# Six of the 24 pieces of a conditioning matrix taken among the first four projection groups of a two-block transformer kernel

## The chip, the cores and the metric

One core of one Trainium2 chip runs the whole program. The metric is device time in microseconds (us) of one execution, as the median of several runs. Its engines are TensorE (PE, with its weight loads listed apart as PEld), VectorE (DVE), ScalarE (ACT), GpSimd (POOL) and SyncE (SP), whose queue issues nearly all weight transfers. Each engine works through its own queue in order.

## The reference, cut to what matters

256 tokens of width 1024 pass through two blocks in fp32. The first block has an attention mixer and a linear attention (HGRN2), whose outputs are merged, and a mixture of 32 experts. The second block has its own attention, a state-space layer and another 32 experts. What the change touches is how the second block is conditioned on one vector `c`, and the linear attention's forget gate in the first block:

```python
# second block: shifts, scales and gates from the conditioning vector
c_act = silu(c)                                   # 1024 values
mod = c_act @ w_ada + b_ada                       # [1024] x [1024, 6144]
sh1, sc1, g1, sh2, sc2, g2 = split(mod, 6)
h = rmsnorm(x, norm1_g) * (1 + sc1) + sh1         # used in the second block only
...
# first block: linear attention
f = lb + (1 - lb) * sigmoid(f_logit)
log_f, k = log(f), 1 - f
bcum = cumsum(log_f)                              # in chunks of 64 tokens
o = linear_attention(q * exp(bcum), k, v, bcum)
```

`mod` depends on `c` and `w_ada` alone, so its work can be done at any time before the second block.

## The kernel before, in words

**Weights.** `Slots` keeps 20 SBUF buffers of 1 MB. `W.get(key)` hands out a weight tile, `W.done(key)` gives it back and calls `W.pump()`, which starts further loads in the order of first use of the whole program, at most `W.ahead` tiles ahead (6 from L509, 3 from L747). All these loads go through SP's queue. At L1144 and L1199 the first block's mixers give their buffers back and the first experts' weights (`m1w`) are started.

**Order.** The program is written as one sequence; a scheduler in the compiler puts each engine's instructions into an order by priority and by its own idea of durations. The engines then run that order as it stands, so an instruction that turns out late holds what is queued behind it on its engine.

**The first column groups.** After the row norm and a transposition (L533 to L540, result `hTf`), the columns of `w_in` are projected in groups of 256: `f0 f1 hq0 hq1` (L649 to L666, forget gate and query of the linear attention), `hi0 hi1` (its values), `kva0 kva1 kvb0 q0 q1` (the attention's keys, values and queries), all as fp32 matmuls (L567, L576). `prep` fetches one group further than the one asked for. `hgg0 hgg1` and `m00` to `m31` follow as split matmuls (L464). `hg_prep` (L687) prepares operands of the linear attention on DVE, ACT and POOL; `hgrn` (L964) does its matmuls, with `level` (L990) producing `am` on DVE (L1004) and `back` (L1008) using it on PE (L1012). `nsa`, `hgrn` and `fill` are interleaved by `run_all` at L1138.

**The pieces.** `mod` is computed in 24 pieces of 256 columns. `ada(site)` (L587) is called at places of the program that have names; where the name is in `ADA_SITES` (L26) it first calls `ada_flush()` and then takes one piece with `ada_()` (L611) at a priority lowered by 100. A piece multiplies eight slabs of a 1 MB weight tile by the columns of `cact` (= silu(c)) and adds them: on ACT (eight scalings, L621) with three adds on POOL (L622 to L624), or, for the piece numbers in `ADA_DVE`, by eight operations on DVE alone (L616, L618). The sum goes to a tile `ada` with two buffers. `ada_flush` (L595) reduces it over partitions on PE (L602 for the first 16 pieces, L608 for the last 8) and adds the bias on DVE (L604, L609). The flush stands at normal priority at the next site, so a piece's last write waits for the flush of the piece two before it.

**`cact`.** `par2` holds `c` and other parameters; it is loaded behind the row norm (L506). At L655 to L660 `cact` is filled: a POOL copy that depends on the forget gate (L655), a POOL copy of `c`, a Tanh on ACT and two DVE operations. Before, the 24 sites begin with `hi0 hi1`, and pieces 14 to 19 go to DVE.

Of the kernel before, what the change touches and what calls it, by code (L numbers as in the profile page):

```python
# [10 lines left out]
F32 = mybir.dt.float32  # L11
BF = mybir.dt.bfloat16
I32 = mybir.dt.int32
AF = mybir.ActivationFunctionType
OP = mybir.AluOpType
# [7 lines left out]
WB = 20  # L23
CAP1 = 32
CAP2 = 64
ADA_SITES = ("hi0 hi1 kva0 kva1 kvb0 q0 q1 cmpk cmpv hgg0 hgg1 m20 m21 m30 m31 m00 m01 m10 m11 bh0 bh2 bh4 bh6 bn0").split()  # L26
ADA_DVE = range(14, 20)

# [182 lines left out]
def view(tile_, spec_at, name):  # L213
    o, w = spec_at[name]
    return tile_[:, o:o + w]
# [94 lines left out]
def program(ctx: ExitStack, tc, T, out, plan):  # L310
    nc = tc.nc
    R32 = mybir.dt.float32r

    tt, ts, stt = nc.vector.tensor_tensor, nc.vector.tensor_scalar, nc.vector.scalar_tensor_tensor
    act, mm, tr = nc.scalar.activation, nc.tensor.matmul, nc.tensor.transpose
# [58 lines left out]
    par1 = cpool.tile([128, p1n], F32, name="par1")  # L374
    P1 = lambda n: view(par1, p1at, n)
    par2 = cpool.tile([128, p2n], F32, name="par2")
    P2 = lambda n: view(par2, p2at, n)
# [6 lines left out]
    def evac(o, i, scale=None, n=256):  # L384

        a, v = 0.22 + n / 1400.0, 0.07 + n / 960.0
        if eng_bal[0] + a <= eng_bal[1] + v:
            eng_bal[0] += a
            if scale is None:
                nc.scalar.copy(o, i)  # L390
            else:
                act(o, i, AF.Copy, scale=scale)
        else:
            eng_bal[1] += v
            if scale is None:
                nc.vector.tensor_copy(o, i)
            else:
                ts(o, i, scale, None, op0=OP.mult)
# [73 lines left out]
    both = lambda t, f: [f(t[0]), f(t[1])]  # L472


    W.ahead = 1
    W.pump()
    f1x = ExitStack()
    f1c = f1x.enter_context(tc.tile_pool(name="f1c", bufs=1))
    fs = f1x.enter_context(tc.tile_pool(name="f1s", bufs=2))
    pp1 = f1x.enter_context(tc.tile_pool(name="ps1", bufs=8, space=PSUM))  # L480

    def ps():
        return pp1.tile([128, 512], F32, name="ps", tag="ps")

    cst1 = f1c.tile([128, c1n], F32, name="cst1")
    grow = cpool.tile([128, 512], F32, name="grow")
# [16 lines left out]
    r = [row_r(fs, x_sb[:, i], junk[:, i], f"n1{i}", i == 0) for i in range(2)]  # L503
    W.drop()

    for t, n in ((par1, "par1"), (cst1, "cst1"), (par2, "par2"), (grow, "bgate")):  # L506
        nc.gpsimd.tensor_copy(t[:, 0:1], r[0])
        (nc.scalar if n == "par1" else nc.sync).dma_start(t, T[n])
    W.ahead = 6  # L509
# [41 lines left out]
    def used(*names):  # L551
        for n in names:
            del sp[n]
            if n in whole:
                W.done(n)
            else:
                W.drop(2)
        W.pump()
# [10 lines left out]
    def pair_T(n):  # L569

        prep(n)
        p = ps().rearrange("p (a t) -> p a t", a=2)
        for a in range(2):
            for k in range(8):
                if n in whole:
                    mm(p[:, a], sp[n][:, k, 128 * a:128 * a + 128], hTf[:, k], start=a == 0 and k == 0, stop=k == 7, skip_group_check=True)  # L576
                else:
                    mm3(p[:, a], wk(n, k, 128 * a, 128), [hTp[0][:, k], hTp[1][:, k]], a == 0 and k == 0, k == 7)
        return p


    cact = cpool.tile([128, 8], F32, name="cact")
    modp = cpool.tile([128, 4, 8], F32, name="modp")
    ada_next = iter(range(24))
    ada_rest = []

    def ada(site):  # L587
        if site in ADA_SITES:
            ada_flush()
            with tc.high_priority(offset=-100):  # L590
                ada_()
        if site == "end":
            ada_flush()

    def ada_flush():  # L595
        while ada_rest:
            n, t, s = ada_rest.pop()
            v, j = ADA[n]
            p = ps()
            if v in ADA_COLS:  # L600
                for a in range(2):
                    mm(p[:, a:a + 1], t[:, 128 * a:128 * a + 128], s, start=(a == 0), stop=True, skip_group_check=True)  # L602
                c = 8 * ADA_COLS.index(v) + 2 * j
                tt(modp.rearrange("p v k -> p (v k)")[:, c:c + 2], p[:, :2], P2("bada")[:, c:c + 2], op=OP.add)  # L604
            else:
                r, c = 32 * (2 * (v // 5) + j // 2), 256 * (j % 2)
                r, c = slice(r, r + 32), slice(c, c + 256)
                mm(p[r, :256], s.to_broadcast([128, 32]), t, start=True, stop=True)  # L608
                tt(grow[r, c], p[r, :256], grow[r, c], op=OP.add)  # L609

    def ada_():  # L611
        n = next(ada_next)
        w = W.get(("ada", n)).rearrange("p (k c) -> p k c", k=8)
        t = fs.tile([128, 256], F32, name="ada", bufs=2)
        if n in ADA_DVE:
            ts(t, w[:, 0], cact[:, 0:1], None, op0=OP.mult)  # L616
            for k in range(1, 8):
                stt(t, w[:, k], cact[:, k:k + 1], t, op0=OP.mult, op1=OP.add)  # L618
        else:
            for k in range(8):  # L620
                act(w[:, k], w[:, k], AF.Copy, scale=cact[:, k:k + 1])  # L621
            nc.gpsimd.tensor_tensor(w[:, 0:4], w[:, 0:4], w[:, 4:8], op=OP.add)  # L622
            nc.gpsimd.tensor_tensor(w[:, 0:2], w[:, 0:2], w[:, 2:4], op=OP.add)
            nc.gpsimd.tensor_tensor(t, w[:, 0], w[:, 1], op=OP.add)  # L624
        W.done(("ada", n))
        ada_rest.append((n, t, C("ones")[:, 0:1]))
# [15 lines left out]
    fT, qT_h = b_[:, 0], b_[:, 1]  # L642
# [3 lines left out]
    v_h = b_[:, :1024].rearrange("p (i c) -> p i c", i=2)  # L646
    sg = b_[:, 1024:].rearrange("p (h t) -> p h t", h=4)

    for hp in range(2):  # L649
        act(fT[:, 2 * hp:2 * hp + 2], pair_T(f"f{hp}"), AF.Sigmoid)  # L650
        used(f"f{hp}")
    for h in range(4):
        ts(fT[:, h], fT[:, h], lb[:, 4, h:h + 1], lb[:, 3, h:h + 1], op0=OP.mult, op1=OP.add)
    ts(kT_h, fT, -1.0, 1.0, op0=OP.mult, op1=OP.add)
    nc.gpsimd.tensor_copy(cact, fT[:, 0, 0:8])  # L655
    nc.gpsimd.tensor_copy(cact, P2("c"))
    csig = fs.tile([128, 8], F32, name="csig", bufs=1)
    act(csig, cact, AF.Tanh, scale=0.5)
    stt(cact, csig, 1.0, cact, op0=OP.add, op1=OP.mult)
    ts(cact, cact, 0.5, None, op0=OP.mult)  # L660
    act(fT, fT, AF.Ln)
    for h in range(4):
        nc.vector.tensor_tensor_scan(cT[:, h], C1("rst64"), fT[:, h], 0.0, op0=OP.mult, op1=OP.add)
    for hp in range(2):
        evac(qT_h[:, 2 * hp:2 * hp + 2], pair_T(f"hq{hp}"), n=512)
        used(f"hq{hp}")  # L666


    kx = {}
# [10 lines left out]
    q1 = b_[:, :512].rearrange("p (h t) -> p h t", h=2)  # L680
# [56 lines left out]
    for c in range(2):  # L737
        for i in range(2):
            proj_t(f"hi{c}", i, pv[i][:, 256 * c:256 * c + 256], c == 0)
        used(f"hi{c}")  # L740
        next(hgp)
        ada(f"hi{c}")
# [7 lines left out]
    evac(tT[:, :, :S], pair_T("kva0"), n=512)  # L750
    used("kva0")
    ada("kva0")
    gw = P1("gw").rearrange("p (k c) -> p k c", k=8)

# [8 lines left out]
    for i in range(2):  # L763
        p = ps()
        proj_t("kva1", i, p[:, :256])
        evac(k_n[:, i, 0:2, 0], p[:, 0:128].rearrange("p (g d) -> p g d", g=2), n=128)
        evac(v_n[:, i, 0], p[:, 128:256], n=128)
        if i:
            ada("kva1")
# [729 lines left out]
    with tc.tile_pool(name="psm", bufs=1, space=PSUM) as pp, tc.tile_pool(name="m1s", bufs=2) as m1s, \  # L1499
# [164 lines left out]
        for i in range(2):  # L1664
            c = slice(i, i + 1)
# [13 lines left out]
    with tc.tile_pool(name="f2s", bufs=2) as fs, tc.tile_pool(name="f2o", bufs=1) as fo, \  # L1679
# [313 lines left out]
        for j in range(4 + 3):  # L1993
            if j < 4:
                i, h = ih[j]
                out_part(i, h, (6, 7))
                t = fs.tile([128, 512], F32, name="gm")
# [42 lines left out]
    with tc.tile_pool(name="psm2", bufs=1, space=PSUM) as pp, tc.tile_pool(name="m2s", bufs=2) as ms, \  # L2040
# [228 lines left out]
        for i in range(2):  # L2269
            tt(q9[:, 4 + i:5 + i], q9[:, 2 * i:2 * i + 1], q9[:, 2 * i + 1:2 * i + 2], op=OP.add)  # L2270
            r9 = rstd(mo, q9[:, 4 + i:5 + i], D, 1, f"r9{i}")
            for d in range(2):
                c = slice(512 * d, 512 * d + 512)
# [5 lines left out]
def two_blocks(tc, T, out):  # L2279
    plan = program(Blank(), Blank(), Blank(), [])  # L2280
    program(tc, T, out, plan)
# [20 lines left out]
```

## Time and profile before

| | us |
|---|---|
| median of 3 runs | 1885.39 (1881.79 to 1885.49) |
| the profiled execution, its own time | 1893.22 |
| its span, first to last instruction | 1891.4 |
| PE busy | 1667.8 (88%) |
| DVE busy | 674.0 (36%) |
| ACT busy | 352.8 (19%) |
| POOL busy | 159.0 (8%) |
| DMA moved | 683.77 MB, mean 362 GB/s |

The shares of the whole span mix stages with different limits: the mixers of the first block (0 to about 300 us), its experts, the second block's mixers around 800 to 900 us, and its experts. The rows further below are read stage by stage.

### The profile page before, as it was taken

The numbers are of one execution on the slowest core, as the hardware profiler recorded it, in microseconds if no ns is written. First come the engines' busy times: TensorE is split into PE (matmuls) and PEld (weight loads), VectorE is DVE, ScalarE is ACT, GpSimd is POOL, SyncE is SP. The second block draws the span as 40 slices with busy tenths as digits, with TensorE's granted clock in tenths as the row PEclk, the third lists the DMA queues.
The fourth block names the chain that finished last, engine by engine and source line by source line (L and its number), as shares of the span: only waits on it lengthen the run. The fifth ranks groups of instructions, "written<-read, shape, count | busy, mean of one in ns | idle before, by whom it ended". The sixth has DMA issues, their size and how long they took to land. (4 is left out here: it accounts for less than half of the span.)

```text
span 1891.4 us, 27461 instructions
## 1 busy us (share of the span) xinstructions
PE 1667.8 (88%) x11518; PEld 907.1 (48%) x11518; DVE 674.0 (36%) x1415; ACT 352.8 (19%) x847; POOL 159.0 (8%) x147
## 2 busy tenths in 40 slices
PE   9988998977886776698999999999889998899887
PEld 8777867644552442498734333333323333233322
DVE  4886765554320000185522232223222222222221
ACT  3654542111111111154400000000000000000000
POOL 2763320000000000031000000000000000000000
PEclk9989989889997887899999999999999999999998
DMA  9455646999999999825799999999999999999994
GB/s 388 154 184 201 267 171 280 391 393 421 420 420 420 421 420 421 346 94 223 296 385 402 421 421 422 421 421 421 421 421 421 421 421 421 421 421 421 421 422 181
DMA packets 95219, 683.77 MB, mean 362 GB/s; under 512 B 10608, under 2 KB 10992, under 8 KB 12560
## 3 DMA queue, kind: packets, MB, share of 16 engines
q1 hardware_dynamic: 94464, 679.90, 87.9%
q8 instruction: 94, 1.54, 0.3%
q10 hardware_dynamic: 624, 2.03, 0.3%
q14 instruction: 37, 0.30, 0.0%
HBM read 680.84 MB, written 1.05 MB: 361 GB/s over the span
## 5 line engine op out<-in xcount | busy, mean ns | idle before, releaser
L2179 PE MATMUL pab<-wt,xe 128*64 128x512 f32 x2048 | 472.5, 598 | 19.5 <-DMA wt<-in_m2w_dram 18.8
L2179 PEld LDWEIGHTS pab<-wt,xe 128*64 128x64 f32 x2048 | 140.6, 136 | 303.1 <-issue 285.7
L2218 PE MATMUL py<-wt,hdT 128*64 128x512 f32 x1024 | 239.7, 601 | 19.2 <-DMA wt<-in_m2w_dram 16.6
L1610 PE MATMUL pa<-wt,xe 128*32 128x256 f32 x2048 | 153.0, 432 | 31.1 <-DMA wt<-in_m1w_dram 30.8
L2218 PEld LDWEIGHTS py<-wt,hdT 128*64 128x64 f32 x1024 | 69.8, 137 | 161.4 <-issue 110.2
L2192 DVE TENSOR_SCALAR gc<-pab 128x512 f32<-128x512 f32 x32 | 22.1, 692 | 340.2 <-PE pab L2185 340.2
L1610 PEld LDWEIGHTS pa<-wt,xe 128*32 128x32 f32 x2048 | 71.1, 120 | 102.2 <-DMA wt<-in_m1w_dram 42.8
L2224 DVE TENSOR_TENSOR b1b<-py,gate 64x512 f32<-64x512 f32 x64 | 44.1, 689 | 201.2 <-PE py L2218 189.3
L2194 ACT ACTIVATE sg<-gc 128x512 f32<-128x512 f32 x32 | 20.1, 630 | 465.1 <-DVE gc L2192 465.1
L1620 DVE TENSOR_TENSOR hid<-pa,sl 128x128 f32<-128x128 f32 x32 | 9.3, 291 | 243.4 <-ACT sl L1618 243.4
L1642 PE MATMUL py<-wt,hdT 128*32 128x256 f32 x1024 | 79.0, 440 | 17.9 <-issue 7.2
L402 POOL TENSOR_SCALAR r<-q 128x1 f32<-128x1 f32 x2 | 0.4, 192 | 953.3 <-DVE q L2270 953.3
L454 DVE TENSOR_TENSOR wh<-wt,wh 128x512 fp32r<-128x512 f32 (+2 forms) x57 | 76.5, 1373 | 10.8 <-ACT wh L452 10.6
L1648 ACT COPY ysb<-py 32x256 f32<-32x256 f32 x128 | 46.4, 363 | 141.9 <-PE py L1642 140.7
L2106 PE MATMUL pm<-b1b,st 128*128 128x512 f32 x120 | 63.7, 632 | 10.3 <-DVE b1b L2224 10.2
L2065 PEld LDWEIGHTS pm<-gt,x_sb 128*128 128x128 f32 x512 | 59.6, 191 | 25.3 <-issue 24.9
L1526 PE MATMUL px<-gt,x_sb 128*128 128x128 f32 x256 | 65.5, 417 | 4.8 <-DVE s5t L1485 1.6
L2107 DVE TENSOR_TENSOR acc<-acc,pm 128x512 f32<-128x512 f32 x60 | 41.3, 688 | 77.6 <-PE pm L2106 77.6
L1526 PEld LDWEIGHTS px<-gt,x_sb 128*128 128x128 f32 x256 | 62.2, 334 | 11.8 <-issue 3.7
L2065 PE MATMUL pm<-gt,x_sb 128*128 128x128 f32 x512 | 65.6, 281 | 1.0 <-DVE gt L2054 1.0
L452 ACT CAST wh<-wt 128x512 fp32r<-128x512 f32 (+2 forms) x65 | 61.9, 1014 | 12.8 <-issue 6.1
L464 PE MATMUL ps<-hTp,wh 128*128 128x256 f32 x480 | 64.0, 295 | 0.0
(581 smaller groups left out, 2000.3 us busy)
## 6 DMA issues: line engine op xcount, KB each, us to landing
wt<-in_m2w_dram SPq DMA_DIRECT2D x384, 1024.0 KB, 19.8
wt<-in_m1w_dram SPq DMA_DIRECT2D x192, 1024.0 KB, 17.7
wt<-in_wf_dram SPq DMA_DIRECT2D x44, 1024.0 KB, 7.9
wt<-in_wada_dram SPq DMA_DIRECT2D x24, 1024.0 KB, 5.0
x_sb<-in_x_dram SPq DMA_DIRECT2D x2, 512.0 KB, 4.2
out_dram<-y SPq DMA_DIRECT2D x4, 256.0 KB, 2.0
wt<-in_b_dram SPq DMA_DIRECT2D x3, 256.0 KB, 8.9
pars<-in_pars_dram ACTq DMA_DIRECT2D x1, 705.0 KB, 8.5
```

Of the source, the lines that this page charges most:

```text
L452: hi = nc.scalar.copy(h[:, a], w[:, a])
L454: lo = e.tensor_tensor(l[:, a], w[:, a], h[:, a].bitcast(F32), op=OP.subtract)
L464: hold(mm(o, a[x], b[y], start=first and j == 0, stop=last and j == 2, skip_group_check=True))
L1526: mm(px[:, k], xkn[:, i, 4 * h + k], gts[g][:, i], start=(k == 0 and i == 0), stop=(i == 1), skip_group_check=True)
L1610: m_ = mm(pa[32 * q:32 * q + 32], xe[:, k], w[:, :, k % 2, 128 * q:128 * q + 128], start=(k == 0), stop=(k == 7), skip_group_check=True)
L1642: mm(py[32 * d:32 * d + 32], hdT[:, 32 * q:32 * q + 32], w[:, q % 2, 256 * d:256 * d + 256], start=(q == 0), stop=(q == 3), skip_group_che ...
L1648: m_copy = nc.scalar.copy(o, i)
L2065: mm(px[:, k], x_sb[:, i, 128 * kk:128 * kk + 128], gts[g][:, i], start=(k == 0 and i == 0), stop=(i == 1), skip_group_check=True)
L2106: mm(p, st2[g][:, i], ysb[g][:, 512 * d:512 * d + 512], start=True, stop=True)
L2179: last = mm(pab[a][64 * h:64 * h + 64], xe[:, k], w[:, 1024 * a + 512 * h:1024 * a + 512 * h + 512], start=(k == 0), stop=False, skip_grou ...
L2218: mm(py[d][64 * d:64 * d + 64], hdT[:, kk % 4, 64 * (kk // 4):64 * (kk // 4) + 64], w[:, kk % 2, 512 * d:512 * d + 512], start=(kk == 0), ...
L2224: tt(ysb[g][64 * e_:64 * e_ + 64, 512 * d:512 * d + 512], py[d][r_], gate2[r_], op=OP.mult)
```

## The change

Six of the 24 pieces are taken at the sites `f1` (three), `hq0` (two) and `hq1` (one), which get calls of `ada`; the sites `hi0 hi1 cmpv hgg0 hgg1 m01` lose theirs. `ADA_DVE` becomes pieces 1, 3, 15, 18 and 19, five in place of six. A site that stands several times in the list takes several pieces, and flushes in between only when more than one is pending. `par2` is loaded at the start, ahead of the first weights, and `cact` is computed ahead of the forget gate from `par2` directly, without the two POOL copies.

```diff
-ADA_SITES = ("hi0 hi1 kva0 kva1 kvb0 q0 q1 cmpk cmpv hgg0 hgg1 m20 m21 m30 m31 m00 m01 m10 m11 bh0 bh2 bh4 bh6 bn0").split()
-ADA_DVE = range(14, 20)
+ADA_SITES = ("f1 f1 f1 hq0 hq0 hq1 kva0 kva1 kvb0 q0 q1 cmpk m20 m21 m30 m31 m00 m10 m11 bh0 bh2 bh4 bh6 bn0").split()
+ADA_DVE = (1, 3, 15, 18, 19)
...
+    nc.sync.dma_start(par2, T["par2"])
     W.ahead = 1
     W.pump()
...
-    for t, n in ((par1, "par1"), (cst1, "cst1"), (par2, "par2"), (grow, "bgate")):
+    for t, n in ((par1, "par1"), (cst1, "cst1"), (grow, "bgate")):
...
     def ada(site):
-        if site in ADA_SITES:
-            ada_flush()
+        for j in range(ADA_SITES.count(site)):
+            if not j or len(ada_rest) > 1:
+                ada_flush()
             with tc.high_priority(offset=-100):
                 ada_()
...
+    csig = fs.tile([128, 8], F32, name="csig", bufs=1)
+    act(csig, P2("c"), AF.Tanh, scale=0.5)
+    stt(cact, csig, 1.0, P2("c"), op0=OP.add, op1=OP.mult)
+    ts(cact, cact, 0.5, None, op0=OP.mult)
     for hp in range(2):
         act(fT[:, 2 * hp:2 * hp + 2], pair_T(f"f{hp}"), AF.Sigmoid)
         used(f"f{hp}")
+        ada(f"f{hp}")
...
-    nc.gpsimd.tensor_copy(cact, fT[:, 0, 0:8])
-    nc.gpsimd.tensor_copy(cact, P2("c"))
-    csig = fs.tile([128, 8], F32, name="csig", bufs=1)
-    act(csig, cact, AF.Tanh, scale=0.5)
-    stt(cact, csig, 1.0, cact, op0=OP.add, op1=OP.mult)
-    ts(cact, cact, 0.5, None, op0=OP.mult)
     act(fT, fT, AF.Ln)
...
         evac(qT_h[:, 2 * hp:2 * hp + 2], pair_T(f"hq{hp}"), n=512)
         used(f"hq{hp}")
+        ada(f"hq{hp}")
```

## Rows read from the trace of the kernel before

**Rows 1.** Busy time by stretch: width, engines' busy us (instructions), granted clock, DMA share, GB/s.

```profile
0.00:20.00 20.00, 17.57 (x85) 16.86 (x86) 4.30 (x15) 5.39 (x8) 3.05 (x12) 1.00 0.92 371
20.00:40.00 20.00, 20.00 (x95) 17.60 (x94) 7.76 (x12) 4.95 (x7) 6.82 (x7) 1.00 1.01 417
...
80.00:100.00 20.00, 20.00 (x97) 16.15 (x96) 6.67 (x18) 12.44 (x29) 15.69 (x12) 1.00 0.56 204
...
280.00:300.00 20.00, 19.20 (x135) 16.02 (x132) 9.79 (x16) 7.42 (x8) 0.00 (x0) 1.00 0.16 56
...
500.00:600.00 100.00, 78.73 (x987) 46.35 (x983) 17.37 (x56) 15.45 (x49) 0.00 (x0) 0.93 1.01 420
```

**Rows 2.** Timeline of SP's queue: start us, us, what; the experts' loads restart.

```profile
296.33 49.38 SPq L259 DMA_DIRECT2D wt<-in_m1w_dram  x20
```

**Rows 3.** Waits of PE, 43 to 165 us: us in total, times, longest us.

```profile
PE ps L602 <- POOL ada L624: 3.6, 2, 2.1
...
PE ps L1012 <- DVE am L1004: 7.1, 1, 7.1
PE ps L1047 <- DVE dgh L1044: 4.7, 1, 4.7
```

**Rows 4.** Timeline of PE: start us, us, what; in brackets idle time before it.

```profile
15.59 27.79 PE L576 MATMUL ps<-hT,wt 128*128 128x256 f32 x128
...
59.31 0.60 PE L602 MATMUL ps<-cst,ada 128*128 128x1 f32 x4 [2.12 <-POOL ada L624]
...
68.41 0.61 PE L602 MATMUL ps<-cst,ada 128*128 128x1 f32 x4 [1.47 <-POOL ada L624]
68.88 8.84 PE L567 MATMUL ps<-wt,hT 128*128 128x256 f32 x32
...
77.92 7.15 PE L567 MATMUL ps<-wt,hT 128*128 128x256 f32 x32
...
110.86 0.27 PE L979 MATMUL ps<-qx,kf 128*64 128x64 f32 x1
...
136.32 8.04 PE L464 MATMUL ps<-hTp,wh 128*128 128x256 f32 x48
...
161.67 6.02 PE L464 MATMUL ps<-hTp,wh 128*128 128x256 f32 x48
```

**Rows 5.** What a piece costs: ACT's part, POOL's three adds (108 to 146 us), DVE's operation.

```profile
108.36 3.30 ACT L621 ACTIVATE wt<-wt,cact 128x256 f32<-128x256 f32 x8
...
L622 POOL TENSOR_TENSOR wt<-wt 128x1024 f32<-128x1024 f32 x4 | 10.0, 2499 | 10.0 <-ACT wt L621 8.8 <-DVE wh L454 1.1
L623 POOL TENSOR_TENSOR wt<-wt 128x512 f32<-128x512 f32 x4 | 5.3, 1316 | 0.0
L624 POOL TENSOR_TENSOR ada<-wt 128x256 f32<-128x256 f32 x4 | 3.1, 785 | 2.5 <-PE ps L602 2.4
...
L618 DVE SCALAR_TENSOR_TENSOR ada<-wt,cact,ada x42: 454/484/2052, 182.1 to 236.2; 128x256 f32<-128x256 f32 x42
```

**Rows 6.** The stretch of PE's longest gap: busy time, then single instructions of DVE and POOL.

```profile
121.00:134.60 13.60, 6.51 (x167) 5.88 (x166) 13.60 (x17) 7.89 (x17) 9.45 (x8) 0.86 0.26 83
...
119.78 0.28 DVE L718 TENSOR_TENSOR qx<-kc 128x128 f32<-128x128 f32 x1
...
119.99 2.77 POOL L622 TENSOR_TENSOR wt<-wt 128x1024 f32<-128x1024 f32 x1 [0.42 <-ACT wt L621]
...
120.45 2.46 DVE L718 TENSOR_TENSOR qx<-kc 128x128 f32<-128x128 f32 x1
...
129.17 2.42 DVE L718 TENSOR_TENSOR qx<-kc 128x128 f32<-128x128 f32 x1
...
133.86 0.68 DVE L1004 TENSOR_TENSOR am<-ps,cst 96x512 f32<-96x512 f32 x1
```

**Rows 7.** Timeline of POOL: the linear attention's memsets, and a last add held long.

```profile
33.62 5.98 POOL L673 MEMSET kx<- 128x2048 f32 x3
...
239.07 2.77 POOL L624 TENSOR_TENSOR ada<-wt 128x256 f32<-128x256 f32 x1
```

## The prediction, on record before the changed kernel was run

> **What bounds the kernel now.** I read the stretches first, then SP's queue, then PE's waits and its timeline, and last DVE and POOL inside PE's gaps. In the experts' stage the DMA engines are busy the whole time (share 1.01 at 420 GB/s between 500 and 600 us), while PE has 21 us of idle time in 100 [rows 1]. That stage's length is given by its bytes, so it moves as a whole with the moment at which its loads start. They start at 296.33 us [rows 2]; just before, the DMA engines are almost idle (56 GB/s, share 0.16, between 280 and 300 us) [rows 1], since the mixers still hold the buffers. So whatever the first block's mixers (0 to 296 us) gain or lose goes over to the end of the program one for one. Nothing behind them is touched by the change.
>
> Inside the mixers PE is the longest queue: 20.00 us of 20 in two of the stretches shown [rows 1]. A gain there can come only from PE's gaps and from the slower clock behind them; PE's own work stays, as every piece keeps its flush. Three gaps matter here: two flushes at 59.31 and 68.41 us that wait for a piece's last add on POOL (2.12 and 1.47 us, 3.6 together) [rows 3, 4], one of 7.1 us before L1012 that waits for `am`, and one of 4.7 us before L1047 [rows 3]. Behind a gap the same matmuls run longer: 32 of L567 take 8.84 us at 68.88 against 7.15 at 77.92, and 48 of L464 take 8.04 at 136.32 against 6.02 at 161.67 [rows 4], so 1.7 and 2.0 us more. The mean granted clock across the 7.1 us gap is 0.86 [rows 6], a mixture of the full and the half level.
>
> **The change part by part.** A piece costs ACT 3.30 us and POOL 2.50 + 1.32 + 0.79 = 4.6 us, or DVE eight operations of 0.48, 3.9 us [rows 5]. Its flush costs PE about 0.5 us wherever it stands (from the flush at 68.41 to the next matmul at 68.88 [rows 4]).
>
> *Pieces 0 to 5 among f1, hq0, hq1.* From 20 to 40 us ACT is busy 4.95 us, DVE 7.76 and POOL 6.82 of 20 [rows 1]. The new work there is four pieces on ACT and POOL (13.2 and 18.4 us) and two on DVE (7.8 us), spread over some 27 us. It fits, if the weights come in time. PE passes four equal groups from 15.59 in 27.79 us [rows 4]: f1 ends at 29.5, hq0 at 36.4, hq1 at 43.4. The DMA engines move 371 GB/s in the first 20 us and 417 after that [rows 1], that is 7.42 MB by 20 us. Each group and each piece is one tile of 128 x 2048 fp32 numbers, 1.05 MB. In the new order of first use the queue carries `x` 1.05, `cst` 0.37, `par2` 0.18, f0, f1, hq0, then pieces 0, 1, 2, then 1.09 MB of constants, hq1, pieces 3 and 4, hi0, piece 5, hi1. Piece 0 is there at 5.8 MB, 16 us; pieces 1 and 2 at 18.6 and 21; hq1 at 10.0 MB, 26 us, ten before PE wants it; pieces 3 and 4 at 29 and 31; hi0 at 34, also ten early. So no group starves; a transfer in front of it costs nothing while those ten us last. `par2` ahead of f0 shifts f0 by 0.4 us; f0 is there at 2.65 MB, well before 15.59.
>
> Ready times: piece 0 on ACT to 19.4 and POOL to 24, flushed at 29.5; piece 1 on DVE by 23; piece 2, whose last add must wait for piece 0's flush, by 31, flushed at 36.4; piece 3 on DVE by 34, flushed at 43.4. Piece 4 is tight: weights at 31, ACT to about 35, then POOL, where the linear attention's memsets take 5.98 us around the same time [rows 7]: 35 + 4.6 is 40, behind the memsets 46, and its flush is due at 43.4. Bounds: nothing, or one wait as long as the longest measured, 2.1 us, with 1.7 us of slow clock, 3.8. I take 1.5 us, nearer to the lower end since it needs the unlucky order of two operations. The Tanh moves ahead of the first sigmoid where ACT is idle; with the two POOL copies away the cost is nothing.
>
> What hides the delay of the forget gate's chain (DVE and ACT now share the stretch with pieces): its first user on PE is L979 at 110.86 us [rows 4], and DVE is busy only 6.67 of the 20 us from 80 to 100 [rows 1]. This cover of 13 us would have to go before a delay counts.
>
> *Sites hi0 and hi1 lose theirs.* The two flush waits at 59.31 and 68.41 belong to the pieces of these two sites. Bounds: 3.6 us at least if only the waits go, 5.3 with the slow matmuls at 68.88; nothing if the next pieces are pulled into their place and wait in the same way. I take 4.
>
> *Sites cmpv, hgg0, hgg1 lose theirs.* This is the stretch of the 7.1 us gap. Between 121 and 134.6 us DVE is busy 13.60 of 13.60 us, PE 6.51 [rows 6]: DVE decides. The operation waited for, L1004 at 133.86, lasts 0.68 us; it is late because of what stands before it. Part of that is POOL's doing: L718 takes 0.28 us at 119.78 and 2.46 at 120.45, where an add L622 of 2.77 us runs beside it, and 2.42 at 129.17 [rows 6]. Two such operations are 2.2 + 2.1 = 4.3 us of DVE time. Four pieces pass POOL between 108 and 146 us (four of each add, 18.4 us) [rows 5]; after the change the sites leave about two (m20's piece and part of the next, which may run ahead by one site). Bounds: nothing (the two remaining pieces hit the same operations) to the whole gap with its slow matmuls, 9.1. I take 6, near the 4.3 us of the two held operations plus most of the 2.0 of clock.
>
> The Trainium skill, "SBUF — State Buffer", section "SBUF: two separate sides", says that VectorE and GpSimd share a pair of ports that the instruction that starts first holds to its end, the other being blocked fully. The two rows of L718 agree (0.28 against 2.46 us beside an add of 2.77). The rule also speaks against this change: the adds moved in front can hold the forget gate's DVE operations, and these can hold the adds.
>
> *Site m01, and DVE's pieces.* Three pieces fewer on DVE after 180 us (11.7 us), two more on ACT and POOL there (6.6 and 9.2 us). Where a gap follows, either sign is possible; bounds one ACT piece, 3.3 us, either way; I take 0. The 4.7 us gap before L1047 is a chain of single steps, and I leave it.
>
> Sum: 4 + 6 - 1.5 = 8.5 us. The profiled execution took 1893.22 us (span 1891.4), so 1884.7. It lies 0.42% above the median of 1885.39; in that ratio the median becomes 1876.9, **1877 us**. From the bounds the forecast's own range is 1885.39 - (5.3 + 9.1 + 3.3), 1868, to 1885.39 - 3.9, 1881.5.
>
> **The rivals.** (1) *More than the gaps above.* With POOL freer the 4.7 us gap and the clock behind it go too, and DVE's three pieces fewer open the later gaps: 14.4 + 4.7 + 3.3 = 22 us, 1863. Against it: that gap is a chain through ACT, POOL and DVE in which POOL was not queued. Chance 0.10.
> (2) *The gain is given back.* PE reaches L1012 some 5 us earlier, DVE's backlog does not shrink, and the wait for `am` grows by what the hi flushes gave; or the pieces are ordered late in the front and land among hg_prep after all, so that the change does not do what it says. DVE's 13.60 of 13.60 speaks for it, the two held L718 against it. Time 1885, within 3.8 us either way. Chance 0.20.
> (3) *Slower: PE waits in its gapless stretch.* PE has no gap from 15.59 to 57 us. Five flushes now stand there or right behind, each a place where PE's order can meet a last add on POOL that is not there yet: a last add L624 took 2.77 us at 239.07 where its mean is 0.79 [rows 5, 7]. At 2.1 us and 1.7 us of clock each, as measured for the hi flushes, four such waits are 15.2 us against 10 of gain: 1885.4 + 5.2 = 1891. It decides from the third wait on, and only where POOL ends a piece after its group has left PE, for which the ready times above leave 5 us in three cases of four. Chance 0.15.
>
> Forecast 0.55.
>
> **How the numbers follow.** A measurement of this kernel tells about 0.2%, 3.8 us, from no change. Faster: 0.55 + 0.10 = 0.65; within: 0.20; slower: 0.15. The range takes the forecast's 1868 to 1881.5, most of rival 2 up to its upper end, and the near part of rivals 1 and 3: 1866 to 1889. What is left out is rival 1's far half and rival 3.
>
> **What would show it.** Right: no wait of PE for POOL between 43 and 75 us; the wait for `am` under 3 us; L718 mostly at 0.3 us between 110 and 135; PE without gaps up to 57 us; the experts' loads restarting near 288 us. Wrong: flush waits between 29 and 45 us, matmuls of f1 to hi1 longer than 7 us a group, `am` as late as before, or the loads restarting where they did. A difference that arises behind the restart would be outside this working altogether.

## The result, and the profile after

The changed kernel takes 1912.22 us (median of 6 runs, 1908.31 to 1915.06) against 1885.44 of the kernel before (6 runs, 1881.79 to 1886.41). The ratio is 1.0139, with a 95% interval of 1.0126 to 1.0151: slower by some 27 us, where 8.5 us less was forecast. The profiled execution of after took 1913.36 us (span 1911.5).

The front of the kernel is where it happens. First PE's waits (in all, times, longest), in two stretches: 15 to 43 us, and from 43 to 165 us. They answer to [rows 3].

```profile
PE ps L604 <- DVE ada L620: 6.5, 1, 6.5
...
PE ps L604 <- POOL ada L626: 12.0, 1, 12.0
PE ps L604 <- DVE ada L620: 5.3, 1, 5.3
PE ps L1014 <- DVE am L1006: 2.7, 1, 2.7
```

L604 is the flush, L620 DVE's operation of a piece, L626 POOL's last add (L602, L618 and L624 of before). The two hi waits of 3.6 us are gone and the 4.7 before L1047 are there still further on. The 7.1 us for `am` have become 2.7; a second wait for `am` behind 165 us has grown from 2.0 to 3.5, so that of 9.1 us in the two 6.2 are left. In their place stand three waits of 23.9 us in all, every one for a piece. PE's timeline of after (start us, us, what, in brackets the idle time before it) shows where; it answers to [rows 4].

```profile
15.82 13.98 PE L577 MATMUL ps<-hT,wt 128*128 128x256 f32 x64
36.31 1.87 PE L604 MATMUL ps<-cst,ada 128*128 128x1 f32 x8 [6.51 <-DVE ada L620]
38.04 8.65 PE L577 MATMUL ps<-hT,wt 128*128 128x256 f32 x32
46.52 0.50 PE L604 MATMUL ps<-cst,ada 128*128 128x1 f32 x4
46.89 7.15 PE L577 MATMUL ps<-hT,wt 128*128 128x256 f32 x32
66.08 1.01 PE L604 MATMUL ps<-cst,ada 128*128 128x1 f32 x4 [12.04 <-POOL ada L626]
72.41 0.98 PE L604 MATMUL ps<-cst,ada 128*128 128x1 f32 x4 [5.32 <-DVE ada L620]
73.25 16.70 PE L568 MATMUL ps<-wt,hT 128*128 128x256 f32 x64
...
104.42 7.15 PE L568 MATMUL ps<-wt,hT 128*128 128x256 f32 x32
...
156.65 7.49 PE L464 MATMUL ps<-hTp,wh 128*128 128x256 f32 x48
```

Before, the 128 matmuls of f0 to hq1 ran without a gap and ended at 43.4 us [rows 4]. Now the group of hi0 starts at 73.25, 29.9 us later. The rows add up to it: waits 6.5 + 12.0 + 5.3 = 23.8; the flushes up to the next matmul 1.7 + 0.4 + 1.0 + 0.8 = 3.9; the 32 matmuls behind the first wait 8.65 us instead of a quarter of 27.79 [rows 4], 1.7 more; and a start 0.2 later; 29.6 together. Behind 73.25 the 64 matmuls of hi0 and hi1 take 16.70 us where 64 of the same size take 13.98 at 15.82, another 2.7.

The busy time by stretch of after (columns as in [rows 1]) shows the same hole, and what it does to the loads.

```profile
20.00:40.00 20.00, 13.49 (x59) 11.62 (x58) 9.26 (x19) 9.05 (x20) 10.69 (x7) 0.86 1.02 420
40.00:60.00 20.00, 14.04 (x65) 11.99 (x63) 19.42 (x34) 17.27 (x39) 15.62 (x13) 0.93 0.83 344
60.00:80.00 20.00, 8.60 (x27) 7.32 (x28) 13.94 (x19) 4.89 (x13) 16.11 (x12) 0.53 0.44 158
...
300.00:320.00 20.00, 19.20 (x136) 15.58 (x134) 9.79 (x20) 6.10 (x8) 0.00 (x0) 1.00 0.12 40
```

From 60 to 80 us PE is busy 8.60 us of 20, at a mean granted clock of 0.53, near the half level (1.2 GHz). The stretch with almost idle DMA engines, 280 to 300 us before [rows 1], is now 300 to 320, and SP's queue goes on with the experts' loads at 317.8 us, against 296.33 [rows 2]. The experts' stage starts some 20 us later and, bound by its bytes, ends later by as much. The first matmul of the experts' gather (L1526 before, L1528 after), the landmark for the end of the mixers in all that follows, starts at 355.0 us against 333.5 in the profiled execution of before. So of the 29.9 + 2.7 us lost in the front, 11 come back by 355 us, and they come back where the gain was forecast: behind hi0 and hi1 the third group starts 26.5 us later than before (104.42 against 77.92 [rows 4]), behind the gap for `am` the L464 20.3 us later (156.65 against 136.32).

Why do the pieces come late? Single instructions of after, in order of time, on ACT, DVE and POOL. L656 is the forget gate's sigmoid, L637 an Exp for `lb` (the gate's lower bound), L623 the eight scalings of a piece, L638 an operation for `lb`, L662 the logarithm, L724 and L732 are operations of `hg_prep`.

```profile
22.93 0.60 ACT L656 ACTIVATE fq<-ps 128x512 f32<-128x512 f32 x1 [5.72 <-PE ps L577]
23.43 4.88 ACT L623 ACTIVATE wt<-wt,cact 128x256 f32<-128x256 f32 x12
...
30.34 1.69 ACT L623 ACTIVATE wt<-wt,cact 128x256 f32<-128x256 f32 x4
32.04 1.28 ACT L637 ACT_TABLE_LOAD   x1
33.34 0.21 ACT L637 ACTIVATE lb<-lb 128x8 f32<-128x8 f32 x1
40.73 1.28 ACT L662 ACT_TABLE_LOAD   x1 [7.18 <-DVE modp L606]
...
47.73 3.29 ACT L623 ACTIVATE wt<-wt,cact 128x256 f32<-128x256 f32 x8
```

```profile
20.01 0.35 DVE L618 TENSOR_SCALAR ada<-wt,cact 128x256 f32<-128x256 f32 x1 [2.77 <-DMA wt<-in_wada_dram]
...
33.58 0.88 DVE L638 TENSOR_TENSOR lb<-lb 128x4 f32<-128x4 f32 x1 [6.64 <-ACT lb L637]
34.38 0.47 DVE L620 SCALAR_TENSOR_TENSOR ada<-wt,cact,ada 128x256 f32<-128x256 f32 x1
...
34.89 1.37 DVE L620 SCALAR_TENSOR_TENSOR ada<-wt,cact,ada 128x256 f32<-128x256 f32 x1
...
61.91 6.47 DVE L724 TENSOR_TENSOR qx<-qx,fq 128x128 f32<-128x128 f32 x6
68.31 3.96 DVE L620 SCALAR_TENSOR_TENSOR ada<-wt,cact,ada 128x256 f32<-128x256 f32 x2
```

```profile
51.09 3.74 POOL L624 TENSOR_TENSOR wt<-wt 128x1024 f32<-128x1024 f32 x1 [4.38 <-ACT wt L623]
...
60.42 2.51 POOL L732 TENSOR_TENSOR kx<-kx,kc 128x256 f32<-128x256 f32 x2
62.90 2.39 POOL L624 TENSOR_TENSOR wt<-wt 128x1024 f32<-128x1024 f32 x1
65.26 0.77 POOL L626 TENSOR_TENSOR ada<-wt 128x256 f32<-128x256 f32 x1
```

- Piece 0's scalings start on ACT at 23.43, right behind f0's sigmoid. ACT had stood idle for 5.72 us ahead of that sigmoid, and the piece's weights had landed at 17.5, as that time began. The order in ACT's queue decides, not its load. Piece 2 follows in the same way; its last add then waits another 1.48 us for the flush of piece 0, whose buffer it writes, and ends at 38.2.
- Piece 1 starts on DVE at 20.01. Five of its seven L620 are done by 27 us (rows left out); the last two stand behind L638, which waits 6.64 us for ACT's Exp, which itself stands behind two sigmoids and piece 2. Piece 1 ends at 36.26; its flush starts at 36.31. It is first in PE's queue after f1, as `ada_flush` takes the youngest pending piece first, so piece 0, ready at 31.3, is flushed behind it. The weights of hq0 had landed at 15.0: PE waits with its next matmuls at hand.
- Piece 4's scalings come at 47.73, behind the logarithm and the exponentials, though ACT had idled from 33.5 to 40.7 and the weights had landed at 33.4. Its adds then stand among `hg_prep`'s on POOL, with a part of piece 5 ahead of the last one, which ends at 66.0: the wait of 12.0.
- Piece 3 goes the same way on DVE: its last two operations stand behind six L724 that take 6.47 us. It ends at 72.3: the wait of 5.3.

No wait of PE in the front is for a transfer. For pieces 0 to 2 e8_ahead below tests this reading; for pieces 3 to 5 it rests on the order of these rows.

### The profile page after: what moved, and what is told of

Same layout as the page of the kernel before. It is cut to its first block, busy times and chain, and to the rows that moved or that the text cites. A ratio compares the mean times of both kernels' runs of the same rounds, so it can differ in the third digit from the quotient of the medians.

```text
span 1911.5 us, 27454 instructions
## 1 busy us (share of the span) xinstructions
PE 1672.7 (88%) x11518; PEld 911.7 (48%) x11518; DVE 660.3 (35%) x1407; ACT 356.1 (19%) x855; POOL 164.8 (9%) x147
## 5 line engine op out<-in xcount | busy, mean ns | idle before, releaser
L1528 PE MATMUL px<-gt,x_sb 128*128 128x128 f32 x256 | 65.2, 412 | 3.0 <-ACT s5v L1348 1.4
L1528 PEld LDWEIGHTS px<-gt,x_sb 128*128 128x128 f32 x256 | 62.2, 334 | 10.1 <-DVE xe L1529 2.6
L464 PE MATMUL ps<-hTp,wh 128*128 128x256 f32 x480 | 65.4, 299 | 0.0
```

The lines of the kernel that those rows point to most:

```text
L464: hold(mm(o, a[x], b[y], start=first and j == 0, stop=last and j == 2, skip_group_check=True))
L1528: mm(px[:, k], xkn[:, i, 4 * h + k], gts[g][:, i], start=(k == 0 and i == 0), stop=(i == 1), skip_group_check=True)
```

## The experiments

Times of all runs, with the kernel before run beside each on the same chip. The last column is the landmark named above, from the profiled execution. Three executions of the kernel before give 333.5, 332.4 and 329.4 us for it, so single executions scatter by some 4 us.

| kernel | median us (runs) | ratio to before | gather starts, us |
|---|---|---|---|
| after | 1912.22 (6) | 1.0139 (1.0126 to 1.0151) | 355.0 |
| e1_late_flush | 1891.66 (10) | 1.0034 (1.0018 to 1.0050) | 332.7 |
| e2_own_bufs | 1907.43 (1) | 1 run | 350.4 |
| e3_front_act | 1910.98 (4) | 1.0137 (1.0105 to 1.0168) | 356.9 |
| e4_cact | 1884.75 (10) | 0.9996 (0.9979 to 1.0013) | 332.1 |
| e5_left_out | 1876.99 (8) | 0.9954 (0.9938 to 0.9970) | 323.3 |
| e6_three | 1876.89 (6) | 0.9956 (0.9938 to 0.9974) | 319.6 |
| e8_ahead | 1880.32 (5) | 0.9961 (0.9946 to 0.9975) | 323.3 |
| b2_before, b3_before | 1883.11, 1884.58 | the kernel before | 332.4, 329.4 |
| e9_late_again | 1886.52 (1) | 1 run | 332.9 |

The theory: PE's queue runs in order, so a flush among the front groups stops PE for as long as its piece is late, and the pieces are late since the queues of ACT, DVE and POOL put them behind work that waits. Rivals: the two shared buffers of `ada`, DVE's pieces by themselves, the earlier `par2` and `cact`, or a gain that was never there.

**e1_late_flush.** After, with the flushes taken out of the front: the six pieces go to a tile of their own, and are flushed two by two, the oldest first, at `kva0`, `kva1` and `kvb0`. The tile takes one of the 20 weight buffers until the queries are projected.

```diff
-            if not j or len(ada_rest) > 1:
-                ada_flush()
+            if site not in ("f1", "hq0", "hq1"):
+                ada_flush(2)
...
-        t = fs.tile([128, 256], F32, name="ada", bufs=2)
+        t = early[:, n] if n < 6 else fs.tile([128, 256], F32, name="ada", bufs=2)
```

> The changed kernel, but the six early pieces write to a tile of their own and their flushes on PE come later: two at kva0, two at kva1, two at kvb0 (and from there two at each site). Nothing else is moved. Theory A (the change costs what PE waits for at the flushes between 29.8 and 72.4 us: 6.5 + 12.0 + 5.3 = 23.9 us, with some 5 us of slower matmuls behind them): PE runs without a gap from 15.8 to about 58 us, and the time is 1872 to 1884 us. Theory B (the pieces' work on ACT, DVE and POOL delays the forget gate's chain, which is 4 us later than before at its first DVE operation, and everything behind it): the late flushes change little, 1900 us or more, with PE waiting for the linear attention's operands instead.

1891.66 us. The front has no gap again; PE's timeline of this kernel:

```profile
15.41 27.79 PE L577 MATMUL ps<-hT,wt 128*128 128x256 f32 x128
43.04 13.98 PE L568 MATMUL ps<-wt,hT 128*128 128x256 f32 x64
```

and the gather starts at 332.7, 22.3 us earlier than in after. In the medians 20.6 of the 26.8 us are back. The flushes moved together with the tile of their own; e2_own_bufs, which has the tile alone, is 4.8 us under after in its one run, so the place of the flushes by itself accounts for some 16 to 21 us. But the gain is not there either, and 1891.66 lies outside both of the expected ranges: three pieces still run between 47 and 74 us among `hg_prep`, PE waits 5.1 us for L810, a flush and L568 up to 110 us, and `am` still costs 7.6 us in two waits, where it cost 9.1 before.

**e2_own_bufs.** After, with the own tile for the six pieces but the flushes left where they are: only the coupling through two buffers goes.

```diff
-        t = fs.tile([128, 256], F32, name="ada", bufs=2)
+        t = early[:, n] if n < 6 else fs.tile([128, 256], F32, name="ada", bufs=2)
```

> The changed kernel, with a tile of their own for the six early pieces instead of the two shared buffers; all flushes where the change has them. Theory A (the flushes stand where the pieces can't be done yet): the waits stay, 20 us or more between 29 and 73 us, time 1905 to 1914. Rival (two buffers, each held until the flush of the piece two before, keep the pieces back): the waits halve, 1895 to 1900.

1907.43 us in one run. PE's waits, 15 to 110 us:

```profile
PE ps L605 <- POOL early L627: 21.9, 2, 20.7
PE ps L605 <- DVE early L621: 5.3, 1, 5.3
```

27.2 us of waits where after had 23.8: the buffers are not the cause. The wait of 6.5 us became 1.2, as piece 1 now ends at 24 us, ahead of the `lb` operations; that for piece 4 grew from 12.0 to 20.7. It ends when piece 4 is ready (68.6 us here, 66.0 in after), whenever PE arrives.

**e3_front_act.** After, with pieces 1 and 3 on ACT and POOL as well.

```diff
-ADA_DVE = (1, 3, 15, 18, 19)
+ADA_DVE = (15, 18, 19)
```

> The changed kernel, with pieces 1 and 3 on ACT and POOL like the other four, none of the six on DVE. Theory A in the form that DVE's pieces are to blame, as their eight dependent operations lie between those of the forget gate: the waits of 6.5 and 5.3 us go, the one of 12.0 us for POOL stays, 1895 to 1903 us. Theory A in the form that any engine is too late, since six flushes in the front come before six pieces can be done: the waits go over to POOL, which has 9.2 us more to do, and the time is 1908 to 1925 us.

1910.98 us, as after. The waits, 15 to 110 us, have gone over to POOL:

```profile
PE ps L604 <- POOL ada L626: 26.0, 2, 18.1
```

So DVE is not at fault by itself; whichever engine takes the pieces, they end late.

**e4_cact.** Before, with only `par2` loaded first and `cact` computed ahead of the forget gate.

```diff
+    nc.sync.dma_start(par2, T["par2"])
...
-    nc.gpsimd.tensor_copy(cact, fT[:, 0, 0:8])
-    nc.gpsimd.tensor_copy(cact, P2("c"))
...
```

> The kernel before, with only the early load of par2 and the early Tanh and cact of the change; all sites and engines of the pieces as before. Theory A: no part of the loss, 1885 us within 4. Rival: the early load or the further table switch delays the first groups or the forget gate by itself: 1890 us or more.

1884.75 us, no difference that can be told: the interval is 4 us less to 2.5 us more. This part of the change explains nothing of the 27. One thing to see in its profile: its front started 2.8 us later than that of b2_before (18.29 against 15.47), the hi waits were 0.4 us, and by 69 us both stood level. A wait for a piece takes up a delay in front of it.

**e5_left_out.** Before, with the six pieces of `hi0 hi1 cmpv hgg0 hgg1 m01` left out altogether.

```diff
+    nc.vector.memset(modp, 0.0)
...
-            with tc.high_priority(offset=-100):
-                ada_()
+            if site in ("hi0", "hi1", "cmpv", "hgg0", "hgg1", "m01"):
+                next(ada_next)
+            else:
+                with tc.high_priority(offset=-100):
+                    ada_()
```

> The kernel before, with the six pieces of hi0, hi1, cmpv, hgg0, hgg1 and m01 left out (their loads, products and flushes; 6 of 24 pieces of the second block's modulation are not computed). It measures what taking these pieces away from their places is worth, apart from where they go. By the sum of the prediction (4 us at hi0 and hi1, 6 at cmpv to hgg1): 1873 to 1877 us. If DVE's backlog is its own and does not shrink with POOL's adds: 1880 to 1883 us, the hi waits alone. If the gain is larger than the two terms: 1865 us.

1876.99 against 1884.57 us: 7.6 us, what the old places of the six pieces cost, together with their six flushes, 0.4 to 0.5 us each, which this kernel leaves out too. Its PE timeline where before had the gap of 7.1 us:

```profile
123.17 1.16 PE L1016 MATMUL ps<-cst,am 96*128 96x128 f32 x8 [2.89 <-DVE am L1008]
124.09 5.99 PE L464 MATMUL ps<-hTp,wh 128*128 128x256 f32 x48
```

The gap is 2.89 instead of 7.1, and the matmuls behind it take 5.99 instead of 8.04 us [rows 4]: 4.2 + 2.0 us. Two things make that less: in b2_before the same 48 matmuls take 6.99 us, so that the second term is 1.0 to 2.0 from execution to execution, and the next wait for `am` is 3.3 us where it was 2.0. The gain exists. Of the 10 us of the two terms 7.6 are seen, with the flushes in them.

**e6_three.** Three pieces only, at `f1`, in place of those of `hi0`, `hi1` and `hgg0`; the own tile, and flushes from `kva0` on, at most two a site. DVE takes piece 1 and pieces 14 to 19.

```diff
-ADA_SITES = ("f1 f1 f1 hq0 hq0 hq1 kva0 kva1 kvb0 q0 q1 cmpk m20 m21 m30 m31 m00 m10 m11 bh0 bh2 bh4 bh6 bn0").split()
-ADA_DVE = (1, 3, 15, 18, 19)
+ADA_SITES = ("f1 f1 f1 kva0 kva1 kvb0 q0 q1 cmpk cmpv hgg1 m20 m21 m30 m31 m00 m01 m10 m11 bh0 bh2 bh4 bh6 bn0").split()
+ADA_DVE = (1, 14, 15, 16, 17, 18, 19)
...
+                ada_flush(2)
```

> Three pieces at f1 instead of six at f1, hq0, hq1 (those of hi0, hi1 and hgg0 move, those of cmpv, hgg1 and m01 stay), flushes at kva0 and kva1, tile of their own. If what is left of the loss with late flushes (7 us over before, 15 over the kernel that leaves the six pieces out) comes from pieces 3 to 5, whose weights land at 28 us and later and which run on into the linear attention's preparation: 1878 to 1884 us. If it comes from the first three, which delay the forget gate's chain by 4 to 5 us: 1887 us or more.

1876.89 us, 9.5 us under the kernel before run beside it, and as fast as with six pieces left out, though every flush is done. It is below the range expected if pieces 3 to 5 make what is left of the loss, and far from the 1887 us of the other theory. That speaks for pieces 3 to 5, but which pieces left their old places, and DVE's share, changed as well. PE's timeline:

```profile
15.11 27.79 PE L577 MATMUL ps<-hT,wt 128*128 128x256 f32 x128
42.73 13.98 PE L568 MATMUL ps<-wt,hT 128*128 128x256 f32 x64
56.55 7.07 PE L577 MATMUL ps<-hT,wt 128*128 128x256 f32 x32
63.45 0.95 PE L605 MATMUL ps<-cst,early 128*128 128x1 f32 x8
...
120.61 0.61 PE L605 MATMUL ps<-cst,ada 128*128 128x1 f32 x4
121.07 1.14 PE L1016 MATMUL ps<-cst,am 96*128 96x128 f32 x8
...
138.73 0.80 PE L1051 MATMUL ps<-dgh,qx 128*128 128x128 f32 x2 [8.70 <-DVE dgh L1048]
```

PE has no gap up to 110 us; the gap for `am` is gone (L1016 follows at 121.07), and part of it comes back before L1051, 8.70 us where 4.7 stood [rows 3]. The forget gate's scans start at 45.31 us here against 40.32 in before, five later, in the fastest kernel of the study.

**e8_ahead.** e6_three, with the three pieces taken ahead of f0's sigmoid in the program.

```diff
-ADA_SITES = ("f1 f1 f1 kva0 kva1 kvb0 ...
+ADA_SITES = ("f0 f0 f0 kva0 kva1 kvb0 ...
...
+    ada("f0")
     for hp in range(2):
         act(fT[:, 2 * hp:2 * hp + 2], pair_T(f"f{hp}"), AF.Sigmoid)
         used(f"f{hp}")
-        ada(f"f{hp}")
```

> As the run with three pieces at f1, but the three are taken ahead of the forget gate's first sigmoid in the program, so that ACT has them between the transposed input and that sigmoid, in the 5.7 us in which it waits for PE, and their weights are loaded ahead of hq0's. If the order on ACT and DVE behind f0's sigmoid is what kept the pieces from the idle time that they were to fill: PE's groups stay without a gap, the forget gate's chain is as early as before (its first DVE operation at 32 to 33 us), 1874 to 1881 us. If DVE's backlog behind 43 us is what counts anyway: the same as the run with three pieces at f1.

1880.32 us; its interval overlaps that of e6_three. What it shows is the ready time. Piece 0 on ACT, and then the last adds of pieces 0 and 2 on POOL, and piece 1's seven L621 on DVE:

```profile
15.71 3.29 ACT L624 ACTIVATE wt<-wt,cact 128x256 f32<-128x256 f32 x8
...
22.93 0.79 POOL L627 TENSOR_TENSOR early<-wt 128x256 f32<-128x256 f32 x1
...
27.71 0.79 POOL L627 TENSOR_TENSOR early<-wt 128x256 f32<-128x256 f32 x1
...
18.01 9.90 DVE L621 SCALAR_TENSOR_TENSOR early<-wt,cact,early 128x256 f32<-128x256 f32 x7
```

Piece 0 is ready at 23.7 us and piece 2 at 28.5, ahead of the end of f1's group near 29.7; in after the last adds of both ended at 31.3 and 38.2. The order in ACT's queue is not all that differs: the three weight tiles are loaded ahead of hq0's here and land at 15.0, 17.5 and 20.0 us, against 17.5, 20.0 and 23.5 in after. That is 2.5 and 3.5 of the 7.6 and 9.7 us; the rest is the order, with 1.5 us of the buffer for piece 2. The forget gate's scans start at 38.35 here, seven us earlier than in e6_three, and the kernel is not faster for it: that chain is not what binds.

**b2_before, b3_before, e9_late_again.** What stayed open after e1_late_flush was its 7 us above before, and whether the two hi waits are there in every execution of before.

> The kernel before once more, for a second trace. Its profiled execution took 1893.2 us, 8.6 above the median of now 23 runs (1884.6), and the two flush waits at 59 and 68 us, 3.6 us together, were not seen in the run with the early cact, whose order on PE is the same. If these waits are there in every execution: 3.6 us again. If they come and go with the moment at which adds on POOL and operations on DVE meet: under 1 us, and a span near 1883.

> The kernel before, a third profiled execution, beside the six pieces flushed late. What stays open is that e1_late_flush is 7 us above before in its median, though in the profiles its first matmul of the gather (L1526 in before, 333.5 and 332.4 us in two executions) starts level, at 332.7. Theory A (the 7 us lie behind the front): the first gather starts at 332 to 334 again, and what differs between executions is the 6.2 us that TensorE's sequencer lost at L426 in the first profile of before and not in the second; this execution shows one of the two, with a span near 1891 or near 1881. Theory B (they lie in the front): the gather starts at 326 or earlier in this execution, 7 us ahead of e1_late_flush.

> e1_late_flush again, the same kernel in another execution. Theory A (the 7 us lie behind the front): the first gather starts at 332 to 334, level with before, and the difference appears between 690 and 790 us, with the 5.6 us of the sequencer at L426 there again. Theory B (they lie in the front): the gather starts 6 to 8 us behind that of the before execution of the same call.

The hi waits are there again in b2_before, 3.6 us with a span of 1881.3, so they are not what made the first execution 10 us longer; in b3_before one is left, 2.2 us. In the three executions of before the gather starts at 333.5, 332.4 and 329.4, in the two of e1_late_flush at 332.7 and 332.9: 1 us later on average, within the scatter. The sequencer's idle time at L426 is in all five (6.2, 4.3, 5.2; 5.6, 5.1), so the idea that it is there in one execution of before and not in another is wrong. From the gather to the second experts' first matmul pass 604.7, 598.4 and 600.7 us in before, 605.1 and 600.2 in e1_late_flush: no steady difference. Neither theory is borne out, and where the 7 us of the medians lie is not settled.

## Why the prediction was wrong

The step that failed is the list of ready times, with the sentence ahead of it, "It fits, if the weights come in time". The weights did come in time (about 2 us later than reckoned: piece 0's at 17.5, piece 4's at 33.4), and the engines did have the idle time that [rows 1] shows. But a piece was let start as soon as its weights and its engine were free, and an engine's queue is an order fixed beforehand.

- **Pieces 0 to 2**: ready by 24, 23 and 31 us, it said. Measured 31.3, 36.3 and 38.2. Pieces 0 and 2 stand behind f0's sigmoid on ACT, piece 1's end behind the `lb` operations that wait for ACT's Exp. e8_ahead, where they stand ahead of the sigmoid and their weights land 2.5 to 3.5 us earlier, has the three at 23.7, 27.9 and 28.5: the durations were about right, the order was not looked at. The price, 0 in the sum, is a wait of 6.5 us with 1.7 us of slower matmuls behind it.
- **Pieces 3 and 4**: by 34 and 40 to 46, it said; measured 72.3 and 66.0, among `hg_prep` on DVE and POOL. The term of 1.5 us with bounds of 0 to 3.8 was 12.0 + 5.3 us of waits and 2.7 of slower matmuls. The bound failed because it was taken from the two hi waits [rows 3], where PE met a piece that was nearly done. Here a whole stage stood ahead of the piece. A wait for something queued behind a stage can be as long as that stage.
- **The flushes**: "about 0.5 us wherever it stands". Behind a gap they took up to 1.0 us each; 3.9 us in the front against 2.5 by that figure.
- **Rival 3** named the mechanism, PE waiting at its front flushes, but priced four waits at 3.8 us, 1891. There were three of 6.5, 12.0 and 5.3. It also trusted the 5 us of slack in the ready times, the step above.
- **The gain, 4 + 6**: right in its places, and roughly in size. In e6_three the third group behind hi0 and hi1 starts at 72.06 us against 76.11 in b2_before, 4.05, of which 0.36 are a front that starts earlier; in b3_before the hi waits are only 2.2 us. In e5_left_out the `am` stretch gives 4.2 and 1.0 to 2.0, of which 1.3 go at the next wait; the whole is 7.6 us in the medians, flushes left out included. In after 11 us came back between 73 and 355 us.
- **The forget gate's cover**: right. The scans start 2.8 us later in after and five later in e6_three, with no wait of PE for them.
- **The transfers and `par2`**: right; no wait for them in the front, and e4_cact is level with before. The experts' loads do not start at 296.33 us, as it says, but go on there (three tiles were issued from 261.7 us on); the sum does not change by that.
- **Site m01**: not measured by itself. The 4.7 us gap was left at its size in after; it grew to 8.70 in e6_three, which no step foresaw.
- **Rival 2**, that DVE's backlog does not shrink: fell with e5_left_out. Its other half, pieces that land among `hg_prep` after all, did happen to pieces 3 to 5.
- **The range**: its upper end, 1881.5, does not follow from the bounds. With nothing gained at the old sites, 3.8 us of waits and 3.3 at m01 they reach 1892.5; the measured 1912.22 lies beyond that too.
- **The port rule**: the prediction held that POOL's adds could hold DVE's operations in front. In e8_ahead seven L621 take 9.90 us, 1.41 each, while POOL's adds run from 19 to 28 us; alone they take 0.48 [rows 5]. By the Trainium skill, "SBUF — State Buffer", section "SBUF: two separate sides", the instruction that starts first keeps the shared pair of ports to its end. An L621 that starts at 24.04 behind an add that runs from 23.69 to 26.22 agrees: it ends at 26.50. Another, which starts 0.03 us ahead of its add, lasts 2.66 us as well: that an operation of DVE waits beside an add is seen here, that the order of starting decides is not. It cost PE nothing there, as the flushes stood later.

Still open: the 7 us of e1_late_flush. Not tried: the flushes in place with all pieces ahead of the sigmoid, six pieces in front that end before `hg_prep` begins, and the pieces of the front at a priority that is not lowered.

## What to carry to other kernels

Idle time of an engine is room for new work only at the place in its queue where the work will stand: for each piece, name the instruction that the compiler's order puts ahead of it, and what that one waits for. A consumer in the order of a gapless engine (here the flush on PE) should stand well behind its producer, or the whole engine pays for the producer's place in another queue; moving work ahead and its consumer along with it are two decisions. Price an unseen wait by the stage that can stand ahead of the producer, not by the longest wait of a kernel in which the order was good.

## What was not expected of the hardware

A small operation of DVE lasted here as long as three memsets of POOL. In e6_three, DVE and POOL:

```profile
35.13 5.20 DVE L642 TENSOR_SCALAR lb<-lb 128x4 f32<-128x4 f32 x1
...
35.02 5.29 POOL L677 MEMSET kx<- 128x2048 f32 x3
```

An operation of four numbers a partition took 5.20 us beside three memsets of 5.29 us in all; in after the same line (L641 there) took 0.17. So the gate's chain starts on L662 at 40.37 us, where its like in before (L653) starts at 32.58. Behind it 2.8 us are made up (L662 and L663 take 1.75 + 0.69 us, their like in before, beside the memsets of [rows 7], 2.99 + 2.25), and the scans are five us late.

Equal kernels differ by up to 10 us in single profiled executions (1893.22, 1883.11 and 1884.58 for before), and the place of the gather by 4: a step of a few us is to be read from the medians, or from landmarks in several executions.
